# Second block of a two-block layer: loads in a written order, the swapped state rows from TensorE, one gelu batch, low weight parts by subtraction

## Chip, cores and metric

One Trainium2 chip, one of its cores. The metric is the device time of one execution in microseconds (us), the median of three runs.

## What is computed

Two transformer-like blocks follow each other on x (512 tokens, 1024 features, float32). The first block is not touched. The second one is, cut to what matters here:

```python
for l in range(DEPTH):
    h = _rms(x, norm1_w[l]) * (1 + sc1) + sh1
    u, q, k, v = jnp.split(h @ w_in[l], [...], axis=-1)
    y_ssm = _s5(u, ...)                       # state space layer, then z * sigmoid(z @ w_glu + b)
    y_attn = _swa_sink(q, k, v, rel_bias, sinks[l])   # 128-token window, 8 heads, 2 KV heads
    mixed = jnp.concatenate([_rms(y_ssm, ...), _rms(y_attn, ...)], axis=-1)
    x = x + g1 * (mixed @ w_out[l])
    h2 = _rms(x, norm2_w[l]) * (1 + sc2) + sh2
    x = x + g2 * _conv_ffn(h2, w_up[l], conv_w[l], conv_b[l], w_down[l])

def _s5(u, ...):        # 32 groups of 16 channels, 64 complex states each
    bu_re = einsum("blgh,gph->blgp", ug, bb_re)   # and bu_im
    s_re, s_im = associative_scan(s[t] = a * s[t-1] + bu[t])   # a complex
    y = einsum(s_re, c_re) - einsum(s_im, c_im) + d_skip * ug
    z = jax.nn.gelu(y)
    return z * jax.nn.sigmoid(z @ w_glu + b_glu)
```

## The kernel before

Features stand on the partitions and tokens in the columns. A product with a weight matrix is made of three float32 products of rounded parts: every weight tile `raw` (128x1024, loaded on SP's queue, two buffers) is split into a rounded part `whi` (ACT copies it, L367) and a rest `wlo`. There are five buffers of each. The rest is made in one of two ways in `load`: VectorE subtracts `whi` from `raw` (L373), or, for the matrices named in `DMA_LO`, ACT writes `-raw` rounded (L370) and a DMA issued by GpSimd reads the weights a second time and adds them to it (L371). The matrices are w5 (projections of the second block), w6 (the GLU), w7 (output projection), w8 (up projection, 44 tiles, read as 128x8x128) and w9 (down projection); before, w6, w7 and w8 have their rest from the DMA.

Between the first block's feed-forward part and the second one's lie the state space layer and the attention. There TensorE's order is written out by hand in `ORDER`, step by step; what the other engines do is put in order by the scheduler from the order in which the steps are written and from its own estimate of their times. The state space steps run over four quarters q of 8 groups: `a` multiplies the inputs `ua` with the table `et` (8 products of 64 columns) and copies the result to `z`, whose upper 64 rows are real parts and lower 64 rows imaginary ones. `b` rotates z by a table of cosines `co` and sines `si` (the sines multiply the rows exchanged between the halves, two instructions of 64 rows each in `crossed`, L1457 and L1458; the cosine product is GpSimd's) and scans (8 scans of 64 columns). `c` rotates back into `sp`. `d` makes y from the tables `tt`, `gt` (two buffers) and sp, copies it to `ys`, writes it to memory as eight small DMAs (`d_z`, half of them issued by SP, half by ACT) and reads it back rearranged as `yt`, to which d times u is added (L1498). `e` is the gelu of yt, which is `zT`, and its split `zhl`, in two batches of two. `g` is the GLU on it, in four parts, and `R` the norm that needs all four.

The attention steps: `kp`, `qp` project, `kt`, `qt` transpose to heads (after a norm of the tokens, `tokn`, on VectorE), `s` makes the scores of one block of 128 queries in two `sc` banks and adds the bias table `relb` on VectorE (L1589), ACT takes the exponentials, `t` transposes, `v` multiplies with the values, `p` is the output projection of the state space part. There are three PSUM banks `acc`, two `sc`, two `tr` and one `po`. `U` is the last projection of u; its copies go to memory (`d_u`) and come back as `ua` through 16 small DMAs of GpSimd.

After that comes `norm_tail` and the second feed-forward part, whose hidden units are made by `hidden2`.

Of the kernel before, what the change touches and what calls it, by code (L numbers as in the profile page):

```python
# [17 lines left out]
P = 128  # L18
# [23 lines left out]
HP = ""  # L42
EG = 0
EN = "avaaavaaaaaaaaaaaaavvvvvvvavavvaaaavaaaaaaaaaaaavaavvvvavvvvaaaavvvvaavvvaaaaavavaaavaavvavvvvvvvvvvavvaavvvvvavvaaavaaaavaaavvaaaaaaavvvvvvvaaaaaaaaavvvavvaavaaaav"
EN_AT = {'k1': (0, 4), 'v1': (4, 4), 'q1': (8, 12), 'h1': (20, 8), 'w1': (28, 8), 's1': (36, 8), 'o1': (44, 16), 't1': (60, 46), 'u2': (106, 4), 'z2': (110, 4), 'y2': (114, 4), 'k2': (118, 2), 'v2': (120, 2), 'q2': (122, 4), 'h2': (126, 12), 's2': (138, 12), 't2': (150, 14)}
ORDER = "U kp0 kp1 a0 a1 kt0 b0 qp0 c0 a2 b1 qp1 kt1 b2 c1 d0 a3 c2 qt0 qt1 b3 c3 d1 s0 qp2 s1 s2 t0 d2 t1 d3 e0 s3 e1 qt2 t2 s4 qp3 v0 t3 s5 v1 g0 qt3 g1 g2 t4 g3 s6 v2 v3 s7 t5 R p0 p1 v4 p2 t6 v5 p3 p4 v6 t7 p5 v7 p6 p7 A"
NW = 16
NHL = 5
SUM_E = "vector"
DMA_LO = ("w6", "w7", "w8")  # L50
LAG = 4
# [3 lines left out]
KSQ = 4  # L55
ZC = "bc"
UL = "gggggggggggggggg"
# [175 lines left out]
def build(tc, I, out, PV, PVN, CS, CSN, CS1, CSN1):  # L233
# [845 lines left out]
    def s5_tables():  # L1079
# [70 lines left out]
        V.tensor_copy(ro_r[:, 0], uc)  # L1150
        V.tensor_copy(ro_i[:, 0], us)
        for n in range(8):
# [237 lines left out]
    def tab(nm):  # L1390
        return bp.tile([P, 1024], F32, tag="tab", bufs=6, name=nm)
# [3 lines left out]

    def s5_load(qs):
        for q in qs:
            ets[q] = tab("et")
            nc.sync.dma_start(ets[q], d_et[q])
            cs[q], ss[q] = wt("co"), wt("si")  # L1400
            nc.sync.dma_start(cs[q], d_rot[q][:, 0])
            nc.sync.dma_start(ss[q], d_rot[q][:, 1])

    def s5_load2(qs):
        for q in qs:
            tts[q] = tab("tt")
            nc.sync.dma_start(tts[q], d_t[q].rearrange("p g x -> p (g x)"))
            gts[q] = bp.tile([P, 8, 9 * 16], F32, tag="tabg", bufs=2, name="gt")
            nc.sync.dma_start(gts[q].rearrange("p g x -> p (g x)"), d_g[q])

    s5_load((0, 1))
    s5_load2((0, 1))
    s5_load((2, 3))

# [32 lines left out]
    def s5_a(q):  # L1447
        pw = acc()
        for g in range(8):
            mm(pw[:, g * 64:g * 64 + 64], ets[q][:, g * P:(g + 1) * P], ua[:, q * 8 + g], True, True)  # L1450
        zs[q] = wt("z")
        copy("z2", q, zs[q], pw)

    def crossed(dst, src, t, sign):

        re, im = slice(0, 64), slice(64, 128)
        V.scalar_tensor_tensor(dst[re], src[im], sign, t[im], op0=ALU.mult, op1=ALU.mult)  # L1457
        V.scalar_tensor_tensor(dst[im], src[re], -sign, t[re], op0=ALU.mult, op1=ALU.mult)  # L1458

    def s5_b(q):  # L1460
        z, z2 = zs[q], wt("z2")
        z2s[q] = z2
        crossed(z2, z, ss[q], 1.0)
        zc = wt("zc")
        (G if "b" in ZC else V).tensor_tensor(zc, z, cs[q], op=ALU.mult)
        V.tensor_tensor(z, zc, z2, op=ALU.add)
        for g in range(8):
            c = slice(g * 64, g * 64 + 64)
            V.tensor_tensor_scan(z2[:, c], mag8[:, q * 8 + g:q * 8 + g + 1].to_broadcast([P, 64]), z[:, c], 0.0, ALU.mult, ALU.add)  # L1469

    def s5_c(q):
        if q == 2:
            s5_load2((2, 3))
        z, z2 = zs[q], z2s[q]
        crossed(z, z2, ss[q], -1.0)
        zc = wt("zc")
        (G if "c" in ZC else V).tensor_tensor(zc, z2, cs[q], op=ALU.mult)
        sp = bp.tile([P, 8, 65], F32, tag="sp", bufs=2, name="sp")
        sps[q] = sp
        V.memset(sp[:, :, 0:1], 0.0)  # L1480
        V.tensor_tensor(sp[:, :, 1:65], z.rearrange("p (g c) -> p g c", g=8),
                        zc.rearrange("p (g c) -> p g c", g=8), op=ALU.add)

    def s5_d(q):
# [6 lines left out]
        ys = wt("ys").rearrange("p (g c) -> p g c", g=8)  # L1491
        copy("y2", q, ys.rearrange("p g c -> p (g c)"), py)
        for t in range(8):
# [7 lines left out]
    def s5_e(n):  # L1501
        if EG and n == 0:
            return
        for q in (range(4) if EG else (2 * n, 2 * n + 1)):
            ge = act(zT[q], zT[q], AF.Gelu_apprx_tanh)
            zz = hl()
            split(zz, zT[q])
            zhl.append(zz)
        tables(ge)
# [139 lines left out]
    def ssm_out(k):  # L1649
# [7 lines left out]

    steps = dict(U=u_last, a=s5_a, b=s5_b, c=s5_c, d=s5_d, e=s5_e, kp=kv_p, kt=kv_t, qp=q_p, qt=q_t,
                 s=swa_s, t=swa_t, v=swa_v, g=glu, R=norm_s, p=ssm_out, A=norm_a)
    with tc.manual_schedule(engines={mybir.EngineType.PE}):  # L1660
        for step in ORDER.split():
            name = step.rstrip("0123456789")
            with tc.high_priority() if name in HP.split(",") else nullcontext():
                steps[name](*([int(step[len(name):])] if step != name else []))
# [93 lines left out]
```

## Time and profile before

| | us |
|---|---|
| median of three runs | 1289.39 |
| lowest, highest | 1288.81, 1290.92 |
| the profiled execution, its own time | 1290.49 |
| its span in the trace | 1288.8 |
| TensorE busy | 1229.4 (95% of the span) |
| VectorE busy | 839.0 (65%) |
| ScalarE busy | 553.6 (43%) |
| GpSimd busy | 319.7 (25%) |
| granted TensorE clock, mean | 0.974 |

The profile shows one execution. PE is TensorE, PEld its weight loads, DVE VectorE, ACT ScalarE, POOL GpSimd, SP the queue that issues most loads. Times in the rows are microseconds from the start of the span unless they are marked ns. The granted clock is a share of 2.4 GHz: 1.00 is the upper level and 0.50 the lower one, 1.2 GHz. A name behind an arrow (<-) is what the engine waited for last.

### The profile page before, as it was taken

The page shows a single profiled execution, that of the slowest core. Times are in us where ns is not written, and L with a number is a line of the kernel's source. Part 1 is how long each engine was busy: PE and PEld are TensorE (multiplying, and loading weights), DVE is VectorE, ACT ScalarE, POOL GpSimd, SP SyncE. Part 2 cuts the span into 40 slices and gives each one's busy share as a digit, 9 for nine tenths or more (in the row PEclk, how much of TensorE's full clock was granted, in tenths as well). Part 3 has the DMA queues.
Part 4 walks back from the last instruction along what each step waited for, and adds up shares of the span by engine and source line. Part 5 has one row for each costly group of instructions (what it writes and reads, how often), then busy time and mean ns, then how long its engine had stood idle before and what let it go on. Part 6 is the DMA issues. An engine that isn't in the chain of part 4 may idle for free.

```text
span 1288.8 us, 17279 instructions
## 1 busy us (share of the span) xinstructions
PE 1229.4 (95%) x6269; PEld 993.2 (77%) x6269; DVE 839.0 (65%) x1617; ACT 553.6 (43%) x917; POOL 319.7 (25%) x403
## 2 busy tenths in 40 slices
PE   6999999999999999999999979889799999999998
PEld 5878766567887888888889878668777788888887
DVE  7667858778977967677568497756547344434362
ACT  5424566453333323232325334765645544444430
POOL 3000002203408384664301231022121211111200
PEclk8999999999999999999999887989899999999999
DMA  6441111115356665656546873556799989796921
GB/s 219 136 135 50 51 33 50 50 41 172 125 177 200 202 213 177 207 182 198 176 142 233 249 181 106 138 135 125 144 205 199 211 166 162 147 178 139 189 82 66
DMA packets 211013, 192.96 MB, mean 150 GB/s; under 512 B 13040, under 2 KB 173696, under 8 KB 210928
## 3 DMA queue, kind: packets, MB, share of 16 engines
q1 hardware_dynamic: 154384, 146.96, 37.6%
q0 software_dynamic: 51456, 40.61, 19.8%
q10 hardware_dynamic: 5088, 4.29, 1.0%
q8 instruction: 50, 0.82, 0.3%
q14 instruction: 35, 0.29, 0.1%
HBM read 178.22 MB, written 15.43 MB: 150 GB/s over the span
## 4 chain that ended last, share of the span: by engine, by line
PE 68%; DVE 6%; issue 3%; DMA 3%; ACT 2%; POOL 1%; POOLq 0%; ACTq 0%; DVEq 0%
PE acc L261 48%; PE sc L261 10%; PE tr L261 8%; DMA wlo<-in_w_dram 2%; DMA raw<-in_w_dram 1%; PE po L261 1%; PE tr L1607 1%; DVE z L1469 1%; DVE wlo L373 1%; DVE z L1458 1%; DVE z L1457 1%; DVE wm L1073 0%; POOL wlo L371 0%; ACT prob L1596 0%; PE tr L932 0%
## 5 line engine op out<-in xcount | busy, mean ns | idle before, releaser
L261 PE MATMUL acc<-hl,whi 128*128 128x512 f32 (+1 forms) x1624 | 482.8, 380 | 11.4 <-ACT whi L367 7.3
L367 ACT ACTIVATE whi<-raw 128x1024 fp32r<-128x1024 f32 (+1 forms) x187 | 194.1, 1040 | 387.9 <-PE acc L261 235.9
L261 PEld LDWEIGHTS acc<-hl,whi 128*128 128x128 f32 x1624 | 294.5, 189 | 78.0 <-issue 8.8
L261 PE MATMUL acc<-hl,wlo 128*128 128x512 f32 (+1 forms) x812 | 308.1, 380 | 1.0 <-DMA wlo<-in_w_dram 1.0
L373 DVE TENSOR_TENSOR wlo<-raw,whi 128x1024 fp32r<-128x1024 f32 (+1 forms) x133 | 174.5, 1314 | 64.4 <-ACT whi L367 61.4
L261 PEld LDWEIGHTS acc<-hl,wlo 128*128 128x128 f32 x812 | 152.9, 188 | 32.8 <-issue 3.8
L371 POOL DMA_DIRECT2D wlo<-in_w_dram x54 | 72.0, 1334 | 323.9 <-ACT wlo L370 214.4
L261 PE MATMUL acc<-hd,whi 128*128 128x512 f32 (+1 forms) x472 | 143.1, 386 | 2.1 <-DVE x L1339 2.1
L261 PE MATMUL acc<-whi,hl 128*128 128x256 f32 (+1 forms) x544 | 109.0, 292 | 1.6 <-ACT tok L248 1.6
L261 PEld LDWEIGHTS acc<-hd,whi 128*128 128x128 f32 x472 | 86.9, 188 | 21.7 <-issue 3.1
L261 PEld LDWEIGHTS acc<-whi,hl 128*128 128x128 f32 x544 | 89.2, 195 | 6.1 <-ACT tok L248 3.0
L261 PE MATMUL acc<-hd,wlo 128*128 128x512 f32 (+1 forms) x236 | 90.9, 385 | 0.0
L1073 DVE CUSTOM_DVE_ANT_0 wm<-wm,cb 128x512 f32<-128x512 f32 x96 | 75.5, 818 | 12.1 <-DMA wm<-in_wmod_dram 12.1
L261 PE MATMUL acc<-wlo,hl 128*128 128x256 f32 (+1 forms) x272 | 78.8, 290 | 0.5 <-DVE wlo L373 0.5
L261 PE MATMUL tr<-hl,whi 128*128 128x512 f32 (+1 forms) x240 | 75.6, 398 | 0.0
L261 PE MATMUL sc<-hl,whi 128*128 128x512 f32 x208 | 64.9, 393 | 0.0
L370 ACT ACTIVATE wlo<-raw 128x1024 fp32r<-128x1024 f32 x54 | 56.5, 1047 | 4.1 <-DMA raw<-in_w_dram 2.2
L920 POOL TENSOR_SCALAR_AFFINE_SELECT keep<-keep 128x128 f32<-128x128 f32 x16 | 9.3, 594 | 186.6 <-ACT keep L914 185.8
L261 PE MATMUL tr<-hl,wlo 128*128 128x512 f32 (+1 forms) x120 | 48.0, 400 | 7.6 <-DMA wlo<-in_w_dram 7.6
L261 PEld LDWEIGHTS acc<-wlo,hl 128*128 128x128 f32 x272 | 53.1, 195 | 2.6 <-DVE wlo L373 1.0
L261 PEld LDWEIGHTS tr<-hl,whi 128*128 128x128 f32 x240 | 46.3, 196 | 10.3
L261 PEld LDWEIGHTS acc<-hd,wlo 128*128 128x128 f32 x236 | 44.3, 188 | 9.4
(424 smaller groups left out, 1962.3 us busy)
## 6 DMA issues: line engine op xcount, KB each, us to landing
raw<-in_w_dram SPq DMA_DIRECT2D x177, 512.0 KB, 4.4
wlo<-in_w_dram POOLq DMA_DIRECT2D x54, 512.0 KB, 7.9
wm<-in_wmod_dram SPq DMA_DIRECT2D x96, 256.0 KB, 4.0
xk<-in_xT_dram SPq DMA_DIRECT2D x16, 256.0 KB, 4.7
d_g<-s5g POOLq DMA_DIRECT2D x4, 576.0 KB, 4.4
gt<-d_g SPq DMA_DIRECT2D x4, 576.0 KB, 5.9
w1c<-in_w1k_dram SPq DMA_DIRECT2D x8, 256.0 KB, 6.4
w1c<-in_w1v_dram SPq DMA_DIRECT2D x8, 256.0 KB, 6.8
```

Source lines behind the costliest of these rows:

```text
L261: nc.tensor.matmul(o, lhsT=l, rhs=r, start=start, stop=stop, **k)
L367: act(hi[:, :m], raw[:, :m], AF.Copy)
L370: act(lo[:, :m], raw[:, :m], AF.Copy, scale=-1.0)
L371: nc.gpsimd.dma_start(v(lo), self.src[:, k0:k1, c0:c1], accum_op=ALU.add)
L373: V.tensor_tensor(lo[:, :m], raw[:, :m], hi.bitcast(F32)[:, :m], op=ALU.subtract)
L920: G.affine_select(g[:, d], g[:, d], fill=1.0, **past)
L1073: V.tensor_tensor_reduce(wm, wm, cb[:, n * 512:(n + 1) * 512], 1.0, 0.0, ALU.mult, ALU.add, mh[:, n, j:j + 1])
L1457: V.scalar_tensor_tensor(dst[re], src[im], sign, t[im], op0=ALU.mult, op1=ALU.mult)
L1458: V.scalar_tensor_tensor(dst[im], src[re], -sign, t[re], op0=ALU.mult, op1=ALU.mult)
L1469: V.tensor_tensor_scan(z2[:, c], mag8[:, q * 8 + g:q * 8 + g + 1].to_broadcast([P, 64]), z[:, c], 0.0, ALU.mult, ALU.add)
L1607: nc.tensor.transpose(tp[:, m * P:(m + 1) * P], probs[n][:, hh, (j - j0) * P:(j - j0 + 1) * P], ident)
```

## The change

Five edits, all in the second block. (1) SP's loads are put into TensorE's written order: `L` loads et, co and si of one quarter, `M` its tt and gt, `W` (`ahead`) the next weight tile; w5 goes ahead of most tables. (2) `a` also makes the rows exchanged between the halves, by 16 products of 64 rows into an `sc` bank, and `b` multiplies both banks with VectorE straight from PSUM; the sign of the sines is put into the table once (L1151). GpSimd keeps only the cosine product of `c`. (3) In `ORDER`, kt0 goes between a0 and a1, and `b1` ahead of `a2`, `c1` ahead of `b2`, `d1` ahead of `c3`. (4) The gelu of all four quarters is one batch (`EG`), behind the copy of the last y on ACT; all four copies of y are ACT's. (5) w8's rest is VectorE's difference.

```diff
-EG = 0
+EG = 1
...
-ORDER = "U kp0 kp1 a0 a1 kt0 b0 qp0 c0 a2 b1 qp1 kt1 b2 c1 d0 a3 c2 qt0 qt1 b3 c3 d1 s0 qp2 s1 s2 t0 d2 t1 d3 e0 s3 e1 qt2 t2 s4 qp3 v0 t3 s5 v1 g0 qt3 g1 g2 t4 g3 s6 v2 v3 s7 t5 R p0 p1 v4 p2 t6 v5 p3 p4 v6 t7 p5 v7 p6 p7 A"
+ORDER = "U L0 kp0 L1 kp1 M0 a0 kt0 a1 b0 qp0 L2 c0 M1 b1 a2 W qp1 W L3 kt1 c1 b2 W d0 a3 W M2 c2 qt0 qt1 b3 d1 c3 M3 s0 qp2 s1 s2 t0 d2 t1 d3 e0 s3 e1 qt2 t2 s4 qp3 v0 t3 s5 v1 g0 qt3 g1 g2 t4 g3 s6 v2 v3 s7 t5 R p0 p1 v4 p2 t6 v5 p3 p4 v6 t7 p5 v7 p6 p7 A"
...
-DMA_LO = ("w6", "w7", "w8")
+DMA_LO = ("w6", "w7")
...
-ZC = "bc"
+ZC = "c"
...
-        V.tensor_copy(ro_i[:, 0], us)
+        V.tensor_scalar(ro_i[:, 0], us, sgn, -1.0, op0=ALU.mult, op1=ALU.mult)
...
-    s5_load((0, 1))
-    s5_load2((0, 1))
-    s5_load((2, 3))
+    def s5_load(q):
+        ets[q] = tab("et")
+        nc.sync.dma_start(ets[q], d_et[q])
+        cs[q], ss[q] = wt("co"), wt("si")
+        nc.sync.dma_start(cs[q], d_rot[q][:, 0])
+        nc.sync.dma_start(ss[q], d_rot[q][:, 1])
+
+    def s5_load2(q):
+        tts[q] = tab("tt")
+        nc.sync.dma_start(tts[q], d_t[q].rearrange("p g x -> p (g x)"))
+        gts[q] = bp.tile([P, 8, 9 * 16], F32, tag="tabg", bufs=2, name="gt")
+        nc.sync.dma_start(gts[q].rearrange("p g x -> p (g x)"), d_g[q])
+
+    def ahead():
+
+        next(p_ for p_ in queue if p_.parts is None).load()
 
...
     def s5_a(q):
-        pw = acc()
+
+        pw, px = acc(), sc()
         for g in range(8):
-            mm(pw[:, g * 64:g * 64 + 64], ets[q][:, g * P:(g + 1) * P], ua[:, q * 8 + g], True, True)
-        zs[q] = wt("z")
-        copy("z2", q, zs[q], pw)
-
-    def crossed(dst, src, t, sign):
-
-        re, im = slice(0, 64), slice(64, 128)
-        V.scalar_tensor_tensor(dst[re], src[im], sign, t[im], op0=ALU.mult, op1=ALU.mult)
-        V.scalar_tensor_tensor(dst[im], src[re], -sign, t[re], op0=ALU.mult, op1=ALU.mult)
+            c, u = slice(g * 64, g * 64 + 64), ua[:, q * 8 + g]
+            mm(pw[:, c], ets[q][:, g * P:(g + 1) * P], u, True, True)
+            for r0 in (0, 64):
+                mm(px[r0:r0 + 64, c], ets[q][:, g * P + 64 - r0:g * P + 128 - r0], u, True, True, skip_group_check=True)
+        zs[q] = pw, px
 
     def s5_b(q):
-        z, z2 = zs[q], wt("z2")
-        z2s[q] = z2
-        crossed(z2, z, ss[q], 1.0)
-        zc = wt("zc")
-        (G if "b" in ZC else V).tensor_tensor(zc, z, cs[q], op=ALU.mult)
-        V.tensor_tensor(z, zc, z2, op=ALU.add)
+
+        pw, px = zs[q]
+        z, z2 = wt("z"), wt("z2")
+        V.tensor_tensor(z, pw, cs[q], op=ALU.mult)
+        V.tensor_tensor(z2, px, ss[q], op=ALU.mult)
+        V.tensor_tensor(z, z, z2, op=ALU.add)
         for g in range(8):
             c = slice(g * 64, g * 64 + 64)
             V.tensor_tensor_scan(z2[:, c], mag8[:, q * 8 + g:q * 8 + g + 1].to_broadcast([P, 64]), z[:, c], 0.0, ALU.mult, ALU.add)
+        zs[q], z2s[q] = z, z2
 
     def s5_c(q):
-        if q == 2:
-            s5_load2((2, 3))
+
         z, z2 = zs[q], z2s[q]
-        crossed(z, z2, ss[q], -1.0)
         zc = wt("zc")
         (G if "c" in ZC else V).tensor_tensor(zc, z2, cs[q], op=ALU.mult)
+        re, im = slice(0, 64), slice(64, 128)
+        V.scalar_tensor_tensor(z[re], z2[im], 1.0, ss[q][im], op0=ALU.mult, op1=ALU.mult)
+        V.scalar_tensor_tensor(z[im], z2[re], 1.0, ss[q][re], op0=ALU.mult, op1=ALU.mult)
         sp = bp.tile([P, 8, 65], F32, tag="sp", bufs=2, name="sp")
         sps[q] = sp
         V.memset(sp[:, :, 0:1], 0.0)
         V.tensor_tensor(sp[:, :, 1:65], z.rearrange("p (g c) -> p g c", g=8),
                         zc.rearrange("p (g c) -> p g c", g=8), op=ALU.add)
+
+    yc = [None]
 
     def s5_d(q):
         ut = wt("ut")
...
             mm(py[:, g * 64:g * 64 + 64], tts[q][:, g * P:(g + 1) * P], ua[:, q * 8 + g], True, False)
             mm(py[:, g * 64:g * 64 + 64], gts[q][:, g, 16:144], sps[q][:, g, 0:64], False, True)
         ys = wt("ys").rearrange("p (g c) -> p g c", g=8)
-        copy("y2", q, ys.rearrange("p g c -> p (g c)"), py)
+        yc[0] = act(ys.rearrange("p g c -> p (g c)"), py, AF.Copy)
...
         for q in (range(4) if EG else (2 * n, 2 * n + 1)):
-            ge = act(zT[q], zT[q], AF.Gelu_apprx_tanh)
+            with tc.issue_after(yc[0].ins):
+                ge = act(zT[q], zT[q], AF.Gelu_apprx_tanh)
...
-    steps = dict(U=u_last, a=s5_a, b=s5_b, c=s5_c, d=s5_d, e=s5_e, kp=kv_p, kt=kv_t, qp=q_p, qt=q_t,
+    steps = dict(L=s5_load, M=s5_load2, W=ahead, U=u_last, a=s5_a, b=s5_b, c=s5_c, d=s5_d, e=s5_e, kp=kv_p, kt=kv_t, qp=q_p, qt=q_t,
-    with tc.manual_schedule(engines={mybir.EngineType.PE}):
+    with tc.manual_schedule(engines={mybir.EngineType.PE, mybir.EngineType.SP}):
```

Three places show how the instructions move. The first is TensorE at the step a0, behind the projection kp1 (et is the table, ua the input):

```order
 L261 MATMUL acc<-wlo,hl 128x256
 L261 MATMUL acc<-whi,hl 128x256
-L261 MATMUL acc<-ua,et 128x64 x16
+L261 MATMUL acc<-ua,et 128x64
+L261 MATMUL sc<-ua,et 64x64 x2
```

Eight products of a quarter become eight of 128 rows and sixteen of 64 rows, taking turns.

The second is VectorE ahead of the first scores, s0, whose bias is added by the rows of L1589. Before:

```order
L1481 TENSOR_TENSOR sp_7225<-z_7062,zc_7223 128x8x64
L1457 SCALAR_TENSOR_TENSOR z2_7242<-z_7211,si_6695 64x512
L1458 SCALAR_TENSOR_TENSOR z2_7242<-z_7211,si_6695 64x512
L1589 ISA prob2_7301,ml_7298<-sc_7302,relb_7295 128x128
L1589 ISA ml_7298 128x1
L1466 TENSOR_TENSOR z_7211<-zc_7245,z2_7242 128x512
```

and now:

```order
L532 TENSOR_TENSOR tokn_7455<-tok_7454,nr_7461 128x512
L1497 SCALAR_TENSOR_TENSOR yt_7364<-ut_7335,pv_82,yt_7364 128x512
L1576 TENSOR_SCALAR relb_7378<-relb_7378 128x1024
L1589 ISA prob2_7384,ml_7381<-sc_7385,relb_7378 128x128
L1589 ISA ml_7381 128x1
```

Before, the scores of s0 stood among the rotations of quarter 3; now they stand behind the addition to yt of quarter 1 (L1497), which has to come back from memory first, and behind the sign change of the bias.

The third is ACT behind the copy of the last y. Before:

```order
L248 ACTIVATE ys_7519<-acc_7502 128x512
L499 ACTIVATE hl_7537<-yt_7292 128x512
L1495 DMA d_z3_3134<-ys_7519 16x8x64 x4
L311 ACT_TABLE_LOAD
L1594 ACTIVATE se_7543<-se_7543 128x4
L1596 ACTIVATE prob2_7544,sl_7542<-prob2_7544,ml_7541 128x256 x4
L1505 ACT_TABLE_LOAD
L1505 ACTIVATE yt_7483<-yt_7483 128x512
L248 ACTIVATE pt_7586<-tr_7581 128x512
L499 ACTIVATE hl_7566<-yt_7483 128x512
L1505 ACTIVATE yt_7529<-yt_7529 128x512
L311 ACT_TABLE_LOAD
```

and now:

```order
L1494 DMA d_z3_3134<-ys_7589 16x8x64 x4
L1596 ACTIVATE prob2_7605,sl_7603<-prob2_7605,ml_7602 128x256 x3
L1505 ACT_TABLE_LOAD
L1505 ACTIVATE yt_7261<-yt_7261 128x512
L1505 ACTIVATE yt_7364<-yt_7364 128x512
L499 ACTIVATE hl_7627<-yt_7261 128x512
L499 ACTIVATE hl_7631<-yt_7364 128x512
L1505 ACTIVATE yt_7553<-yt_7553 128x512
L1505 ACTIVATE yt_7599<-yt_7599 128x512
L499 ACTIVATE hl_7635<-yt_7553 128x512
L499 ACTIVATE hl_7639<-yt_7599 128x512
L311 ACT_TABLE_LOAD
```

The copy `pt` of a transposed tile and the exponentials of the next scores stood between the gelus; now they stand behind the whole batch, whose last gelu needs quarter 3 back from memory.

## Rows read from the trace of the kernel before

**Rows 1.** The page, busy us (share of the span) and instructions.

```profile
PE 1229.4 (95%) x6269; PEld 993.2 (77%) x6269; DVE 839.0 (65%) x1617; ACT 553.6 (43%) x917; POOL 319.7 (25%) x403
```

**Rows 2.** Who waited for whom on PE: us in total, times, longest us.

```profile
PE tr L261 <- DMA wlo<-in_w_dram: 7.6, 2, 5.8
PE sc L261 <- DVE ml L1589: 7.5, 3, 6.0
...
PE tr L1540 <- DVE tokn L532: 6.5, 1, 6.5
...
PE acc L261 <- DMA wlo<-in_w_dram: 1.0, 1, 1.0
```

**Rows 3.** Busy time by stretch: us, PE PEld DVE ACT POOL, PEclk, DMA share, GB/s.

```profile
920.00:1010.00 90.00, 80.82 (x337) 64.50 (x336) 42.78 (x82) 44.85 (x56) 18.70 (x13) 0.94 1.07 206
1010.00:1100.00 90.00, 90.00 (x390) 73.10 (x389) 42.99 (x55) 44.67 (x55) 15.80 (x11) 1.00 0.91 171
```

**Rows 4.** Busy time by stretch: the first feed-forward part, and the second.

```profile
300.00:500.00 200.00, 197.33 (x883) 158.51 (x882) 162.00 (x303) 65.94 (x88) 103.65 (x138) 1.00 0.60 182
930.00:1100.00 170.00, 166.62 (x707) 134.28 (x706) 81.03 (x130) 83.00 (x102) 31.63 (x22) 0.98 0.97 187
```

**Rows 5.** Groups by line and form: busy us, mean ns, idle before.

```profile
L373 DVE TENSOR_TENSOR wlo<-raw,whi 128x1024 fp32r<-128x1024 f32 x123 | 166.1, 1353 | 63.0 <-ACT whi L367 60.0 <-ACT rg L504 2.4
...
L370 ACT ACTIVATE wlo<-raw 128x1024 fp32r<-128x1024 f32 x54 | 56.5, 1047 | 4.1 <-DMA raw<-in_w_dram 2.2 <-PE acc L261 2.0
```

**Rows 6.** Timeline of PE: start us, us, what, count, idle before.

```profile
733.14 5.93 PE L261 MATMUL acc<-ua,et 128*128 128x64 f32 x32 [2.62 <-DMA raw<-in_w_dram]
...
746.04 1.89 PE L261 MATMUL acc<-ua,et 128*128 128x64 f32 x16
...
767.02 1.09 PE L1540 MATMUL tr<-cst,tokn 128*128 128x128 f32 x4 [6.51 <-DVE tokn L532]
...
775.67 1.23 PE L261 MATMUL sc<-k2T,q2T 64*128 64x128 f32 x8
...
783.56 1.94 PE L261 MATMUL sc<-k2T,q2T 64*128 64x256 f32 x8
...
802.06 0.39 PE L261 MATMUL acc<-sp,gt 128*128 128x64 f32 x2
...
842.34 2.07 PE L261 MATMUL sc<-k2T,q2T 64*128 64x256 f32 x4 [6.02 <-DVE ml L1589]
...
846.10 1.49 PE L261 MATMUL sc<-tot_s,cst 128*128 128x512 f32 x2
```

**Rows 7.** Busy time by stretch, around the step d1.

```profile
770.00:780.00 10.00, 10.00 (x54) 9.66 (x54) 7.70 (x24) 0.60 (x1) 3.89 (x3) 0.56 0.38 106
```

**Rows 8.** Groups of PE by form, narrow weights: busy us, mean ns.

```profile
L261 PE MATMUL po<-pt,vtok 128*64 128x128 f32 x88 | 7.7, 284 | 0.0
...
L261 PE MATMUL sc<-s5g,bb 128*16 128x128 f32 x64 | 2.5, 275 | 0.0
```

**Rows 9.** DMA issues by line: KB each, median us to landing.

```profile
yt<-d_z POOLq DMA_DIRECT2D x4, 256.0 KB, 3.0
...
d_z<-ys ACTq DMA_DIRECT2D x16, 32.0 KB, 2.2
```

**Rows 10.** Timeline of ACT: start us, us, what, count, idle before.

```profile
776.45 2.02 ACTq L1495 DMA_DIRECT2D d_z<-ys  x4
...
810.48 0.58 ACT L248 ACTIVATE pt<-tr 128x512 f32<-128x512 f32 x1
...
813.87 1.28 ACT L311 ACT_TABLE_LOAD   x1
...
837.63 1.06 ACT L367 ACTIVATE whi<-raw 128x1024 fp32r<-128x1024 f32 x1 [4.55 <-DMA raw<-in_w_dram]
```

**Rows 11.** Timeline of PE where 64-row products give way to 128-row ones.

```profile
816.12 1.08 PE L261 MATMUL po<-pt,v 128*64 128x256 f32 x8
817.13 0.73 PE L261 MATMUL acc<-hl,whi 128*128 128x512 f32 x2
```

More of the change, by code (lines that the diff above doesn't have):

```diff
@@ L1394, in build @@
     zs, z2s, cs, ss, sps, ets, tts, gts = {}, {}, {}, {}, {}, {}, {}, {}
[L1396 to L1409, printed above, removed]
-    s5_load((0, 1))
-    s5_load2((0, 1))
-    s5_load((2, 3))
+    def s5_load(q):
[11 more added lines that the diff above has]
+        next(p_ for p_ in queue if p_.parts is None).load()
     def u_out(q, ps):
```

## The prediction

> **What bounds the kernel now.** I read the page first: PE is busy 1229.4 us of a span of 1288.8 [rows 1], so 59.4 us of PE idle, and whatever a low clock costs inside the busy time, is all that any edit can win, unless it takes products away; this one adds some. Then the list of who waited for whom on PE: of its largest waits four lie in the second block, 7.6 and 1.0 us for a rest tile that comes by DMA, 7.5 us for the row minimum of the scores and 6.5 us for the normed tokens [rows 2]. The table by stretch shows what the first two cost in all: in 920 to 1010 PE did 337 instructions at a mean granted clock of 0.94, in the next 90 us 390 of the same kind at 1.00 [rows 3]. The timeline of PE shows where the others lie [rows 6]: 6.51 us ahead of the transposes of qt1 at 767.02, and 6.02 us ahead of s7 at 842.34. Around the first, PE is busy but slow: in 770 to 780 the granted clock was 0.56, near the lower level of 1.2 GHz, after the wait [rows 7]. The sum below is made against the profiled execution, 1290.49 us, which is 1.1 us over the median of the runs, 1289.39; I carry the difference over unchanged.
>
> **w8's rest by subtraction: -12.2 us.** Removed: 44 of the 54 ACT instructions of 1.05 us that write -raw [rows 5], 44 issues on GpSimd and 44 tiles of 512 KB read a second time. Added: 44 subtractions on VectorE, 1.35 us each by the mean of its group, 60 us [rows 5]. VectorE was busy 81 of 170 us in 930 to 1100; with about 1.35 us for each of some 26 tiles there it comes to 116 of 170, 68%. In the first feed-forward part, where every rest is already subtracted, VectorE was busy 162 of 200 us and PE 197 of 200 [rows 4]: that load does not hold PE up. What hides the subtractions is thus VectorE's own slack; should it go, each one late costs up to 1.35 us. The two tiles that follow the norm come behind its last instruction on VectorE instead of behind a DMA. The gain is the 53 missing instructions of 920 to 1010 at 90/390 = 0.23 us: 12.2 us, of which 8.6 are waits [rows 2, 3] and the rest mostly low clock. Bounds: -12.2, and -2 if the load of raw itself, two buffers deep, was the real limit. I take the full value, since DMA engines were busy 1.07 there and half of w8's reading goes away.
>
> **The start, 0 us.** SP now brings the next w5 tiles ahead of most tables, but ACT's queue has the issue of the last `d_u` ahead of the second tile of kv, which can hold up kp0 by some 2 us. PE waited 2.62 us ahead of a0 anyway [rows 6], for inputs that go through memory. One covers the other: 0, between -2.6 and +2.
>
> **The exchanged rows on PE: +12.4 us.** 64 products of 64 rows are added, two instructions each as for the others, 128. A full one took 5.93/32 = 0.185 us at the low clock of 733 and 1.89/16 = 0.118 at the high one, a ratio of 1.57 [rows 6]. No row has this shape. From above it is the full one at the low clock throughout, 0.185: 23.7 us. From below it is weights of 16 columns, 2.5/64 = 0.039 each: 5.0 us [rows 8]. Nearest are weights of 64 columns with twice as many columns streamed, 7.7/88 = 0.088 [rows 8]; I take a little less, 0.08. Those of a0 and half of a1, 48, fall where PE was slow: 48 x 0.08 x 1.57 = 6.0; the other 80 cost 6.4. They lie on PE's path, since nothing there waits for another engine now. VectorE loses the two 64-row products of `b` and gains two of 128 rows; with the two copies of z it had and GpSimd's product gone, `b` is shorter.
>
> **The wait at qt1: -10.9 us.** qt0 ended at 767.02 - 6.51 = 760.51, and s0 began at 775.67 [rows 6]: 15.2 us for the 4 transposes of qt1 and the 32 instructions of d1. At 0.118 they need 4.25. In VectorE's new order the rotation of quarter 1 stands behind the norm of qp0 and ahead of the norm of qp1, and PE has kt1, d0 and a longer a3 between qp1 and qt1, so the tokens are there. Bounds: -10.9, and -6.5 if the clock stays low.
>
> **A new wait at s1: +4.3 us.** The scores of s0 hold both `sc` banks until VectorE has added the bias, and that now stands behind the addition to yt of quarter 1. From the end of d1: ACT's copy of y, then a weight tile's two conversions (2.1 us [rows 5]) and the issue of the writes (2.02 [rows 10]), 2.2 us to land, the read back 3.0 [rows 9], and five short instructions (copy, GpSimd's issue, addition, sign of the bias, products of one bank), which I estimate at the 0.58 us of a 128x512 copy on ACT each [rows 10], 2.9: 12.2 us. Before, s1 began 783.56 - 775.67 = 7.9 us after d1 [rows 6], and PE comes there no later now. Queued behind that addition on VectorE are all scores and, through them, t0 and d2. Bounds: 0 (the conversions run earlier), and +9.5 (both transfers take twice as long).
>
> **One gelu batch, and s7: -3.5 us.** The 7.5 us that PE waited for ml [rows 2], 6.02 of them ahead of s7 [rows 6], go nearly whole: ACT stood at 837.63 for 4.55 us before a weight tile that had just been asked for [rows 10], with the split that VectorE needed behind it; in the new order on SP and ACT that tile is asked for several tiles earlier. That is -7.0. But the copy `pt`, at 810.48 before, 8.0 us after the end of d3 (802.45) [rows 6, 10], now stands behind the batch: copy 0.6, issue 2.0, landing 2.2, issue 0.6, landing 3.0, addition 0.6, gelu 0.6, two splits 1.2, all estimates or rows as above, and a table load of 1.28 [rows 10], 12.1; and ahead of it five small instructions for the exponentials of s3, at the same 0.58, 2.9: 15.0 us, 7.0 later. PE's work between covers an unknown part; half is +3.5. Bounds of the whole: -7.0 and +7.0.
>
> **Norm before the second feed-forward part: +0.5 us.** Three subtractions (4.1 us) stand among its chain on VectorE and three conversions leave ACT. VectorE waited for PE and ACT there; I let one eighth through. Bounds 0 and +4.1.
>
> Sum: -12.2 + 0 + 12.4 - 10.9 + 4.3 - 3.5 + 0.5 = -9.4. The profiled execution would take 1281.1 us, the median 1280.0. The forecast's own range is 1272 to 1288.
>
> **Rivals.** (a) *The stage gains in full.* The narrow products run side by side at the lower price (5.0), yt comes back in time (0), and the batch is free (-7.0): -12.2 + 5.0 - 10.9 - 7.0 + 0.5 = -24.6, 1264.8 us. For it: the price of the narrowest weights in rows 8. Against it: VectorE's order is fixed with yt ahead of the scores, and a write and a read back cannot take nothing.
>
> (b) *Slower: PE drains at each change of width.* Full and half products take turns, 64 changes over the four quarters (two per group). If each one waits until the product before it is through, it costs the difference between the length of one and its pitch, 0.284 - 0.088 = 0.197 us [rows 8]: 12.6 us, at the steps a, on PE's path. Then the sum is +3.2, 1292.6 us. It decides against the change from 0.15 us per switch (9.4/64). Against it: where eight half-width products give way to full ones, these start at 817.13, before the 1.08 us from 816.12 are over [rows 11]; one change shows no gap. For it: no row has them taking turns. The Trainium skill, "TensorEngine Tiling (Array Packing)", section "Tiling Modes", Key Properties, says that a change of the tiling mode drains TensorE, and that tiles of one mode work independently; the switch in rows 11 does not show the former at a size that matters, and by the page this change would pay it 64 times.
>
> (c) *The second feed-forward part keeps its wait.* If the stall at its start was that of raw, not of the second read, only 2 of the 12.2 us go: +0.8, 1290.2 us. For it: raw has two buffers. Against it: the first feed-forward part has the same buffers and loses 3 us in 200.
>
> **Chances.** Forecast 0.53, (a) 0.22, (b) 0.15, (c) 0.10. A measurement of this kernel can tell about 0.2%, 2.6 us, from no change. Faster by more than that: nine tenths of the forecast's, all of (a), a tenth or two of (b) and (c), 0.74. Within it: 0.13. Slower: 0.13, nearly all from (b). The range 1264 to 1293 reaches from (a) to (b); outside it are sums at two bounds at once.
>
> **What would show it.** Right: no wait of PE for wlo after the norm, and about 390 instructions in the 90 us that begin w8; a0 to a3 with 0.13 us per half product at first and 0.08 later; no wait at qt1; a wait of about 4 us at s1 put down to ml; t3 waiting for pt, s7 not waiting. Wrong: half products over 0.15 us each at the high clock; PE waiting in the second feed-forward part for VectorE's wlo; or the stage from a0 to R shorter than before by over 10 us.

## Result and the profile after

The changed kernel takes **1304.04 us**, median of 9 runs (1292.46 to 1310.17), beside 1290.34 for the kernel before on the same chips (9 runs, 1288.81 to 1295.84). The ratio is **1.008, 95% interval 1.0055 to 1.0106**: slower by about 10 us (7 to 14). The forecast was 1280.0, faster, with a range of 1264 to 1293; the time lies outside it and the sign is wrong. Times below that come from a ratio are the ratio's distance from 1 times 1290 us.

The two profiled executions, 1305.97 and 1290.49 us, differ by 15.5 us. Where it arises is read from PE's timeline. After:

```profile
734.32 0.33 PE L261 MATMUL acc<-ua,et 128*128 128x64 f32 x2
...
734.85 0.43 PE L261 MATMUL acc<-ua,et 128*128 128x64 f32 x2
735.21 0.34 PE L261 MATMUL sc<-ua,et 128*64 128x64 f32 x4
735.48 0.44 PE L261 MATMUL acc<-ua,et 128*128 128x64 f32 x2
...
776.91 1.97 PE L1540 MATMUL tr<-cst,tokn 128*128 128x128 f32 x8
...
785.53 1.22 PE L261 MATMUL sc<-k2T,q2T 64*128 64x128 f32 x4
789.28 1.19 PE L261 MATMUL sc<-k2T,q2T 64*128 64x128 f32 x4 [2.53 <-DVE z L1460]
804.30 2.49 PE L261 MATMUL sc<-k2T,q2T 64*128 64x256 f32 x8 [5.94 <-DVE ml L1589]
...
848.52 1.97 PE L1607 MATMUL tr<-cst,prob 128*128 128x128 f32 x8 [7.11 <-ACT pt L248]
...
871.75 1.83 PE L261 MATMUL sc<-k2T,q2T 64*128 64x256 f32 x8 [2.80 <-DVE ml L1589]
...
875.27 1.80 PE L261 MATMUL sc<-tot_s,cst 128*128 128x512 f32 x2
```

Against [rows 6]: a0 begins at 734.32, 1.2 us later than before; s0 at 785.53 instead of 775.67, 9.9 later; s1 at 804.30 instead of 783.56, 20.7 later; R at 875.27 instead of 846.10, 29.2 later. So the stretch from a0 to s1 loses 20 us and that from s1 to R another 8. In what follows R, the span gives 13.8 of the 29.2 back (1304.2 against 1288.8 at its end): that is w8, by the stretches of 90 us that begin it, to be held against the 337 and 390 instructions and the clocks of 0.94 and 1.00 in [rows 3]:

```profile
949.00:1039.00 90.00, 90.00 (x397) 73.47 (x397) 68.45 (x109) 41.48 (x54) 0.00 (x0) 1.00 0.55 161
1039.00:1129.00 90.00, 90.00 (x390) 73.14 (x390) 51.71 (x62) 32.79 (x41) 0.00 (x0) 1.00 0.33 96
```

The list of who waited for whom on PE, after, against [rows 2]: the rest by DMA is gone from it, and so is tokn ahead of qt1. The scores' minimum (ml) stands at 8.7 us instead of 7.5; new are pt with 7.1 and z with the 2.53 of the rows above.

```profile
PE sc L261 <- DVE ml L1589: 8.7, 2, 5.9
...
PE tr L1607 <- ACT pt L248: 7.1, 1, 7.1
```

Last the clock. By stretches of 30 us from 760, before:

```profile
760.00:790.00 30.00, 21.06 (x119) 19.12 (x117) 26.52 (x77) 8.40 (x30) 9.53 (x10) 0.70 0.51 148
790.00:820.00 30.00, 28.21 (x189) 25.02 (x188) 22.43 (x73) 21.64 (x51) 1.07 (x2) 0.85 0.32 89
820.00:850.00 30.00, 21.36 (x99) 15.48 (x99) 22.54 (x55) 24.61 (x54) 3.46 (x4) 0.83 0.72 172
```

and after:

```profile
760.00:790.00 30.00, 27.47 (x176) 25.76 (x175) 15.77 (x39) 8.60 (x15) 5.90 (x7) 0.67 0.62 154
790.00:820.00 30.00, 23.45 (x111) 21.04 (x110) 17.30 (x59) 7.80 (x31) 4.19 (x5) 0.61 0.31 96
820.00:850.00 30.00, 21.97 (x121) 19.53 (x120) 13.96 (x40) 11.96 (x31) 1.10 (x2) 0.67 0.44 123
```

The waits are shorter in the first of them (PE busy 27.47 instead of 21.06), yet the clock is lower in all three: behind each new wait PE goes on at 1.2 GHz (granted clock 0.50 from 801.7 to 835.9, from 846.1 to 852.9 and from 873.4 to 876.8). From s2 to the end of d3 the same work took 19.6 us (807.41 to 827.00) instead of 16.4 (786.02 to 802.38).

### The profile page after: what moved, and what is told of

It is laid out like the page before. It is cut to its first block, busy times and chain, and to the rows that moved or that the text cites. A ratio compares the mean times of both kernels' runs of the same rounds, so it can differ in the third digit from the quotient of the medians.

```text
span 1304.2 us, 17370 instructions
## 1 busy us (share of the span) xinstructions
PE 1254.9 (96%) x6397; PEld 1014.8 (78%) x6397; DVE 886.8 (68%) x1658; ACT 507.0 (39%) x868; POOL 251.5 (19%) x355
## 5 line engine op out<-in xcount | busy, mean ns | idle before, releaser
L373 DVE TENSOR_TENSOR wlo<-raw,whi 128x1024 fp32r<-128x1024 f32 (+1 forms) x177 | 232.3, 1315 | 97.9 <-ACT whi L367 93.7
L261 PE MATMUL acc<-whi,hl 128*128 128x256 f32 (+1 forms) x544 | 117.0, 306 | 2.5 <-ACT tok L248 1.6
L261 PEld LDWEIGHTS acc<-whi,hl 128*128 128x128 f32 x544 | 95.8, 210 | 7.4 <-ACT tok L248 3.0
L261 PE MATMUL acc<-wlo,hl 128*128 128x256 f32 (+1 forms) x272 | 82.7, 304 | 1.4 <-DVE wlo L373 1.4
L261 PE MATMUL tr<-hl,whi 128*128 128x512 f32 (+1 forms) x240 | 72.9, 386 | 0.0
L261 PEld LDWEIGHTS acc<-wlo,hl 128*128 128x128 f32 x272 | 57.0, 210 | 3.6 <-DVE wlo L373 2.1
L1339 DVE TENSOR_TENSOR x<-x,acc 128x512 f32<-128x512 f32 (+1 forms) x49 | 31.7, 655 | 22.4 <-PE acc L261 22.3
L261 PEld LDWEIGHTS sc<-hl,whi 128*128 128x128 f32 x208 | 39.1, 188 | 9.0
```

Of the source, the lines that this page charges most:

```text
L261: nc.tensor.matmul(o, lhsT=l, rhs=r, start=start, stop=stop, **k)
L373: V.tensor_tensor(lo[:, :m], raw[:, :m], hi.bitcast(F32)[:, :m], op=ALU.subtract)
L1339: done[0] = V.tensor_tensor(x[k][:, cs], x[k][:, cs], ps[:, cs], op=ALU.add)
```

## Experiments: the parts alone

Four kernels each add one part of the change to the kernel before.

**w8's rest by subtraction.**

```diff
-DMA_LO = ("w6", "w7", "w8")
+DMA_LO = ("w6", "w7")
```

> The kernel before with the one edit that w8's low parts are differences (DMA_LO without w8). Theory: this part does in the second feed-forward part what the term of the prediction says, since the changed kernel's stretch from the end of the norm to the end is 13.9 us shorter than before's; 10 to 15 us faster than before, about 1277 us, and no wait of PE for wlo after the norm. Rival: the gain shows only because the changed kernel comes to this stretch with other loads in flight; then 0 to 5 us faster.

Measured: 1277.75 us, ratio 0.9904 (0.988 to 0.9927), 12.4 us faster. In the 90 us that begin w8 PE issued 405 instructions at full clock, where [rows 3] has 337:

```profile
920.00:1010.00 90.00, 90.00 (x405) 73.78 (x404) 68.56 (x109) 41.05 (x52) 0.00 (x0) 1.00 0.51 156
```

The term stands, at its size.

**The exchanged rows.** The edits to `s5_a`, `s5_b`, `s5_c`, to `ZC` and to the sign of the table, without any other.

> The kernel before with the exchanged rows from the matrix engine alone (loads, order of steps, gelu and w8 as before). Theory A (the loss sits in the rows): 128 instructions at the 0.095 us each that the changed kernel's a0 shows at the high clock, 12 us, and more where the clock falls during them, as it does in a1, a2 and a3 there; with nothing of the wait at qt1 gone, since before's order puts qt1 right behind qt0: 12 to 25 us slower, 1302 to 1315 us. Theory B (the loss sits in the new order and the waits for yt): the shorter b on VectorE gives part of the 6.5 us at qt1 back, so 3 to 9 us slower.

Measured: 1301.18 us, ratio 1.0082 (1.0062 to 1.0103), 10.6 us slower, between the two theories and nearer to A; its interval, 8 to 13, reaches into the ranges of both, so it doesn't decide between them. The wait of 6.5 us at qt1 is gone here too (`b` is shorter on VectorE), and still the sum is a loss.

**The gelu batch.** `EG = 1`, the copies of y on ACT, the gelu behind the last of them.

> The kernel before with the one gelu batch alone (EG=1, the copy of y on ScalarE, gelu issued after the last copy). Theory B (the batch makes t3 wait for the last yt): PE waits 5 to 8 us ahead of t3 for pt and no longer 6.0 us ahead of s7: between 2 us faster and 6 us slower. Theory A (the batch is free): the wait ahead of s7 goes, 4 to 7 us faster.

Measured: 1291.48 us, ratio 1.0002 (0.998 to 1.0023): no difference. PE's waits show both halves of it, 3.3 us for pt ahead of t3 (not there before) and 2.9 in all for ml, where the list before has 7.5:

```profile
PE tr L1610 <- ACT pt L248: 3.3, 1, 3.3
PE sc L261 <- DVE ml L1592: 2.9, 3, 1.7
```

**The loads and the order of steps.** `ORDER`, `L`, `M`, `W` and SP in the written order.

> The kernel before with the fixed order of loads on SP and the new order of steps alone (state rows as before, two gelu batches, w8 as before). Theory A (the loss sits in the rows): the wait at qt1 goes, 5 to 11 us faster. Theory B (the order brings yt of quarter 1 late to the scores): s1 waits 4 to 10 us for ml, and what qt1 gave is lost again: 0 to 10 us slower than before.

Measured: 1305.98 us, ratio 1.0119 (1.0097 to 1.0142): 15.4 us slower, more than either theory gave. Alone it is the dearest part. It holds the loads (1) and the exchanged steps of `ORDER` (3) together; which of the two makes the loss was not tried apart. s0 comes 4.2 us earlier than before (771.48 against 775.67), and s1 9.8 later:

```profile
771.48 1.23 PE L261 MATMUL sc<-k2T,q2T 64*128 64x128 f32 x8
793.35 2.49 PE L261 MATMUL sc<-k2T,q2T 64*128 64x256 f32 x8 [13.17 <-DVE ml L1585]
```

The four parts add up to -12.4 + 10.6 + 0.2 + 15.4 = +13.8 us. The whole change measured 10 (7 to 14). So most of the loss lies in two of the parts, and they can be looked into one by one. Some interplay is left: taken out of the changed kernel, the rows give back about 7 us and an early bias table 3.6 by the ratios (both below), where alone these two are worth 10.6 and 10.3.

## Experiments: what makes the order of loads dear

The search begins with SP's queue. In the kernel before, the scheduler asked for the bias table at 748.0 us, some 28 us ahead of s0:

```profile
747.96 0.33 SPq L1575 DMA_DIRECT2D relb<-in_relb_dram  x1
```

In the written order its load stands where the step s0 stands, behind the tables of quarter 3 (`M3`) and, ahead of these, SP's half of the writes of y of quarter 1, which need ACT's copy of the result of d1. SP is held at these writes; the tables and relb follow without another wait. After:

```profile
786.26 1.94 SPq L1494 DMA_DIRECT2D d_z<-ys  x4
788.51 0.34 SPq L1405 DMA_DIRECT2D tt<-d_t  x1
788.95 0.79 SPq L1407 DMA_DIRECT2D gt<-d_g  x1
789.79 0.42 SPq L1575 DMA_DIRECT2D relb<-in_relb_dram  x1
```

Then yt of quarter 1 is read back. GpSimd can ask for that read only behind the cosine product of c3, which waits for b3's scan. That scan is late because VectorE stood 9.09 us at the clearing of `sp` for quarter 3: `sp` has two buffers, and the one needed comes free when d1 has read quarter 1's. The rest of c2 and all of b3 come behind that on VectorE. VectorE has its sign change of relb and the scores behind the norm of the tokens of qp2 and the addition to that yt. GpSimd's timeline, the DMA issues of relb and of that yt (KB, us to landing) and VectorE's timeline, after:

```profile
791.61 1.71 POOL L1471 TENSOR_TENSOR zc<-z,co 128x512 f32<-128x512 f32 x1 [11.66 <-DVE z L1464]
793.27 0.90 POOL L371 DMA_DIRECT2D wlo<-in_w_dram  x1
793.87 0.86 POOL L1496 DMA_DIRECT2D yt<-d_z  x1
```

```profile
relb<-in_relb_dram SPq DMA_DIRECT2D x1, 512.0 KB, 5.2
...
yt<-d_z POOLq DMA_DIRECT2D x1, 256.0 KB, 5.5
```

```profile
785.68 0.07 DVE L1477 MEMSET sp<- 128x8 f32 x1 [9.09 <-PE acc L261]
...
799.02 0.69 DVE L519 TENSOR_TENSOR nsq<-tok 128x512 f32<-128x512 f32 x1 [3.77 <-ACT tok L248]
...
801.64 0.69 DVE L532 TENSOR_TENSOR tokn<-tok,nr 128x512 f32<-128x512 f32 x1
802.25 0.74 DVE L1497 SCALAR_TENSOR_TENSOR yt<-ut,pv,yt 128x512 f32<-128x512 f32 x1
802.92 0.69 DVE L1576 TENSOR_SCALAR relb<-relb 128x1024 f32<-128x1024 f32 x1
803.73 0.29 DVE L1589 CUSTOM_DVE_ANT_0 prob<-sc,relb 128x128 f32<-128x128 f32 x1
```

The read takes 5.5 us, where the yt row of [rows 9] has 3.0, and is there at about 799.4. The tables had landed by then (the later one at 793.8); beside it travelled the end of relb, a weight tile's rest and two reads of u. VectorE still has the norm of qp2 ahead of the addition, and PE's qp2, which ends at 798.4 and ran at the low clock until 794.9, lets that norm begin only at 799.02. So the scores of s0, all in PSUM by 790.5, begin at 803.73.

Two things thus hold the scores back. relb is there at 795.0, and before that they can't begin; that is the smaller one. VectorE changes its sign only at 802.92, 7.9 us later: that is its place in VectorE's order. In b_loads relb is there at 788.3 and its sign is changed at 791.6, behind a wait of 6.0 us for yt.

The test is to ask for relb earlier and change no other load; since its sign change then comes earlier in the written order too, the scheduler also puts the scores of s0 and s1 ahead of most of the norm and of that addition on VectorE.

```diff
-... W L3 kt1 c1 ...
+... W L3 B0 kt1 c1 ...
...
+    def relb_load(kv):
+        t = tab("relb")
+        relbs[kv] = t.rearrange("p (h y) -> p h y", h=4)
+        nc.sync.dma_start(t, I["relb"][:, kv * 1024:(kv + 1) * 1024])
+        V.tensor_scalar(relbs[kv], relbs[kv], -1.0, None, op0=ALU.mult)
...
-        if i == 0:
-            relbs[kv] = tab("relb").rearrange("p (h y) -> p h y", h=4)
...
+        if i == 0 and kv not in relbs:
+            relb_load(kv)
...
```

> The kernel of b_loads with one step moved: the load of the position bias relb and its change of sign stand behind the load of the last et table instead of at s0, which is behind the tables of quarter 3. Theory C (the order of loads costs because relb, asked for at 748.0 us in the kernel before, is asked for only at 782 to 790, behind tables that wait for buffers until d1 ends, and because VectorE then has the addition to yt ahead of the scores): the wait of 13.2 us for ml ahead of s1 nearly goes, and the kernel is 9 to 15 us faster than b_loads, 1291 to 1297 us. Theory D (it is the slow read of yt itself, 4 to 7 us beside the tables): VectorE still waits for yt ahead of the scores, less than 4 us faster than b_loads.

Measured: 1294.68 us, ratio 1.0039 (1.0021 to 1.0056) against 1.0119 of b_loads: 10.3 us faster, theory C. SP asks for relb at 751.22, and PE's wait ahead of s1 falls from 13.17 to 2.54 us; s1 comes at 784.35, 9.0 earlier than in b_loads:

```profile
784.35 2.34 PE L261 MATMUL sc<-k2T,q2T 64*128 64x256 f32 x8 [2.54 <-DVE ml L1589]
```

The run moves the load and VectorE's order together; what each has of the 10.3 us was not tried apart. The same step in the changed kernel:

> The changed kernel with the same step moved. Theory C: the wait of 5.9 us for ml ahead of s1 goes, and with it the low clock behind it in t0, d2 and d3, 3 us; 6 to 12 us faster than the changed kernel, 1292 to 1298 us; the wait of t3 for pt stays. Theory D: less than 3 us faster.

Measured: 1295.75 us, ratio 1.0052 (1.0027 to 1.0076). By medians that is 8.3 us under the changed kernel, by the ratios 3.6, and the intervals overlap, so the total alone decides little. In the trace s1 comes at 794.40 instead of 804.30, with a wait of 1.83 instead of 5.94. But 5.9 of these 9.9 us stand already at the first products of s0 (779.62 instead of 785.53), ahead of any use of relb: in this run a2 went through at the high clock. From s0 to s1 it is 14.8 us instead of 18.8, so the trace gives the edit 4.0. The wait ahead of t3 stays, 7.8 us.

What is left of b_loads with relb cured, 5 us (3 to 7), was not taken apart. PE shows a wait of 3.4 us ahead of t0 there, and one of 4.6 for tokn ahead of qt1, where the kernel before has 6.5, so the latter isn't it.

## Experiments: what makes the rows dear

In the changed kernel two full products and four half ones take 0.63 us at the high clock (from 734.85 to 735.48, shown above). The full ones took 0.236 [rows 6], so a half one costs 0.1 if it carries the difference. The rival (b) says that it is the change of width. Grouping tells them apart:

```diff
-        for g in range(8):
-            c, u = slice(g * 64, g * 64 + 64), ua[:, q * 8 + g]
+        cu = [(slice(g * 64, g * 64 + 64), ua[:, q * 8 + g]) for g in range(8)]
+        for g, (c, u) in enumerate(cu):
             mm(pw[:, c], ets[q][:, g * P:(g + 1) * P], u, True, True)
+        for g, (c, u) in enumerate(cu):
             for r0 in (0, 64):
                 mm(px[r0:r0 + 64, c], ets[q][:, g * P + 64 - r0:g * P + 128 - r0], u, True, True, skip_group_check=True)
```

> The kernel of b_rows with the products of a step a in another order: the eight of full width first, then the sixteen of half width, so that the width changes twice in a quarter instead of sixteen times. Theory A (a change of width costs): the pair of full products behind the half ones takes 0.36 us instead of 0.236 at the high clock in the changed kernel, 0.124 us at each of 32 groups, so 3 to 5 us faster than b_rows, 1296 to 1298 us. Rival (the alternation costs nothing, the time is that of the columns): within 1.5 us of b_rows. A third: full drains of 0.197 us at 64 changes would give 11 to 12 us.

Measured: 1293.85 us, ratio 1.0028 (1.0016 to 1.0041): 7.0 us faster than b_rows, between the first and the third expectation. PE's timeline of a2 shows the prices apart:

```profile
749.05 1.89 PE L261 MATMUL acc<-ua,et 128*128 128x64 f32 x16
750.87 1.15 PE L261 MATMUL sc<-ua,et 128*64 128x64 f32 x32
751.95 0.39 PE L261 MATMUL acc<-whi,hl 128*128 128x256 f32 x1
```

Start to start, sixteen full ones take 1.82 us and 32 half ones 1.08, each run with the one change of width that ends it. Two full and four half ones that take turns need 0.63 us, with two changes. From these three sums come 0.104 us for a full one, 0.029 for a half one, under the lowest price of [rows 8], and **0.15 us for a change of width**, 9.8 us for 64. The starts inside the runs give nearly the same (a full one every 0.112 us, two half ones every 0.058): 0.145 us for a change, 9.3 for 64. My first expectation had seen only one of the two.

**Without the rows.** The changed kernel with `s5_a` to `s5_c`, `ZC` and the table's sign of before.

> The changed kernel with the state rows as before: crossed products on VectorE, the copy of z, no half products on the matrix engine. If the parts add up as they did alone (rows +10.6 us), 1292 to 1295 us. Rival: in the new order the rows are what takes the wait at qt1 away, and without them it comes back: 1298 us or more.

Measured: 1292.81 us, ratio 1.0024 (1.0011 to 1.0037), about 7 us under the changed kernel, as the parts say. The wait ahead of s1 is 12.1 us here: s0 comes 12.2 us earlier than in the changed kernel (773.38), and s1 10.2 (794.07), since the scores stand behind the same yt there, for which VectorE waits 4.9 us.

## Experiments: cures together, and the batch's place

**Both cures in the changed kernel**, relb early and the products grouped:

> The changed kernel with two cures: relb asked for behind the last et table (as a_relb) and half products behind all full ones of a quarter (as br_grp). If the cures add up: 7 us faster than a_relb, 1287 to 1291 us, about the kernel before. Rival: part of what the grouping gives is taken by the wait for pt ahead of t3 (7.8 us in a_relb), which follows yt and not PE: 1291 to 1294 us.

Measured: 1283.88 us, ratio 0.9933 (0.9909 to 0.9957): 8.6 us faster than the kernel before, better than expected. From a_relb it is 15.4 us by the ratios, 11.9 by the medians and 7.3 in the profiled spans (1291.5 and 1284.2), so what the grouping is worth here stays open between 7 and 15. In the trace the grouped products ran at the high clock in all four a steps, 2.9 us each. The wait for pt ahead of t3 stays at 7.9.

**w8 and the batch, without the rest:**

> The kernel before with two parts of the change: w8's low parts as differences and the one gelu batch. Parts that add up (-12.4 and +0.2 us alone): 1276 to 1280 us, not to be told from b_w8. Rival: the batch's wait for pt ahead of t3 (3.3 us in b_eg) is hidden or its gain at s7 (6.0 to 1.7 us) counts more once the weights come as differences: 1272 to 1275 us.

Measured: **1275.16 us, ratio 0.9874 (0.9853 to 0.9894)**, the lowest median of the study, between my two expectations: 16.3 us (14 to 19) under the kernel before. It is not surely under b_w8, whose interval overlaps.

**The batch behind t2.** t3 waits because the copies of t2 stand behind gelus that wait for the last yt. ACT, in the changed kernel:

```profile
844.88 0.63 ACT L1505 ACTIVATE yt<-yt 128x512 f32<-128x512 f32 x1 [6.05 <-DVE yt L1497]
845.42 1.13 ACT L499 ACTIVATE hl<-yt 128x512 fp32r<-128x512 f32 x2
846.57 1.28 ACT L311 ACT_TABLE_LOAD   x1
847.87 0.60 ACT L248 ACTIVATE pt<-tr 128x512 f32<-128x512 f32 x1
```

```diff
-... e0 s3 e1 qt2 t2 s4 ...
+... e0 s3 qt2 t2 e1 s4 ...
```

> The kernel of bw_eg with the gelu batch one place later in the order of steps, behind t2 instead of ahead of it, so that both copies pt of t2 stand ahead of the batch on ScalarE and VectorE. Theory (t3 waits because those copies stand behind a batch that waits for the last yt): the 3.3 us ahead of t3 go, 2 to 5 us faster than bw_eg, and the best of all, 1272 to 1276 us. Rival (the batch is then late for the gate's products): a wait of PE for hl ahead of g0 takes the place of t3's, within 1.5 us of bw_eg.

Measured: 1281.29 us, ratio 0.992 (0.9893 to 0.9948), 5.9 us slower than bw_eg. A miss: the wait ahead of t3 falls from 3.55 to 1.42 us, but 6.41 ahead of s7 are back, for the reason that [rows 10] show before: ACT stands before a weight tile (4.93 us, raw at 842.81) with what VectorE needs behind it.

```profile
816.97 1.06 PE L1610 MATMUL tr<-cst,prob 128*128 128x128 f32 x8 [1.42 <-DVE prob L1602]
...
847.51 2.07 PE L261 MATMUL sc<-k2T,q2T 64*128 64x256 f32 x4 [6.41 <-DVE ml L1592]
```

> The kernel of a_relb_grp with the gelu batch behind t2 in the order of steps. Theory as for bw_eg_t2: the wait of 7 to 8 us for pt ahead of t3 goes, 4 to 8 us faster than a_relb_grp, 1280 to 1286 us, faster than before but not than b_w8. Rival: g0 waits for hl instead, within 1.5 us.

Measured: 1283.2 us, ratio 0.9926 (0.9899 to 0.9952), the same as a_relb_grp. The 7.9 us ahead of t3 are 1.4 now, and 3.7 appear ahead of s5 for ml; R comes at 853.77 instead of 853.17. The rival's size held, not its place. That stretch does not end with the one wait that is largest in it.

## Why the prediction was wrong

**The step that failed is "A new wait at s1: +4.3".** It took 12.2 us from the end of d1 to s1, bounded at +9.5 by twice the transfers. The trace has 18.8 (785.5 to 804.30), against 7.9 before: +10.9, beyond its bound. No other term came out dearer than its dear bound. The direction and the queue were right (the scores behind the addition to yt on VectorE), but four things were left out. VectorE stood 9 us in front of the clearing of `sp` for quarter 3, with c2 and b3 behind it, so GpSimd, behind c3's product, issued the read only at 793.87, some 3 us after the writes were there (issued by 788.2, 2.2 us to land). The read then takes 5.5 us instead of 3.0. The norm of qp2, which stood ahead of the addition in the order I showed, holds the addition up to 802.25. And relb, asked for 42 us later than before, is there only at 795.0, so that scores ahead of the norm could not have begun before that either. bl_relb shows relb's place together with VectorE's order to be worth 10.3 us alone, and a_relb some 4 in the changed kernel; the others are read from the trace and were not tried alone. The start's term counted what SP's new order brings forward and not what it puts back.

**Exchanged rows, +12.4.** Right in sum, by luck. The four steps took 21.9 us instead of 9.2, +12.7. But a half product costs 0.03 us at the high clock, not 0.08, and some 9.5 us are changes of width. Rival (b)'s mechanism was there at about 0.15 us per change instead of 0.197, at the very price from which I had it decide; I had put the two in different cases, while the nearest row's price happened to cover half products and changes alike. The 0.185 us that I took as a full product's price at the low clock is a mean over a stretch whose clock fell only at 734.4; in d1, at 0.50, it was 0.214. Since the sum of the term came out, this is not why the forecast failed. I had judged the switch in [rows 11] by the overlap alone; the pair of products behind it takes 0.73 us, the next such pair 0.64, so some 0.1 us was there to be seen:

```profile
817.93 0.64 PE L261 MATMUL acc<-hl,whi 128*128 128x512 f32 x2
```

br_grp shows that a change costs time here. The Trainium skill's page "TensorEngine Tiling (Array Packing)", section "Tiling Modes", says that a change of the tiling mode drains TensorE. With that br_grp agrees in the cost; it does not show what TensorE does meanwhile.

Not in the term at all: `px` holds a bank of `sc` until VectorE has multiplied it, and s0 waits 2.5 us for that (1.5 in b_rows, 4.2 in a_relb_grp); in the changed kernel that product too stands behind the clearing of `sp`.

**The wait at qt1, -10.9.** The 6.5 us are gone, but qt0's and qt1's transposes and d1 (776.91 to 785.53) run at the low clock, 0.214 us an instruction in d1. With half of the 1.8 us of transposes qt1's, 7.7 us remain of 15.2: -7.5, near the bound of -6.5 and not the value taken.

**One gelu batch, -3.5.** In the changed kernel t3's wait grew by 7.1 and s7's (0.94 and 6.02) fell to 2.8: +2.9, within the bounds. Alone the part is worth nothing either way. Half of t3's wait covered by PE was a guess, and nothing covered it.

**w8, -12.2,** held (-12.4 alone, some 13.8 behind R). **The start, 0,** held: +1.2, with 0.9 us each for whi and wlo at kp0, as feared. **The norm, +0.5,** held: R to the first product behind the norm took 57.0 before (846.10 to 903.07) and 57.1 after (875.27 to 932.35).

The clock between the steps was put at nothing, without a reason; this is the other step that failed. There qp0 and qp1 took 16.3 us instead of 12.2, being behind the a steps during which it fell, and s2 to d3 3.2 us more. With these 7.3 us, which are read from one trace of each kernel, +10.9 in place of +4.3, -7.5 in place of -10.9 and +2.9 in place of -3.5, the sum of -9.4 becomes +14, close to the 15.5 between the profiled executions.

## What to carry to other kernels

When a load queue goes from a scheduler's order to a written one, list every load on it and compare when each is asked for before and after, above all those that the written steps mention only at their use. Then look where the scheduler puts the instructions that use them on the other engines: here relb came 42 us later on SP, but was there 7.9 us before VectorE's turn came to it, and moving both forward gave back 10.3 us in b_loads. When products of two widths are needed, issue each width in one run (7.0 us here). And a wait that was removed came back here at the next thing that PE waits for: in bw_eg_t2 t3's fell to 1.42 us and 6.41 stood ahead of s7.

## What the runs showed of the hardware

Half-width products (weights of 64 columns, 64 streamed) in a run take 0.029 us each at the high clock, less than a third of a full one (0.104 to 0.112); a change between the widths takes about 0.15 us there. At the low clock 32 of them with the change behind take 1.90 us (a1 of br_grp, granted clock 0.50) instead of 1.08. The granted clock fell to its lower level within runs of such small products although PE was never idle in them: in the changed kernel inside a1, a2 and a3. In a1 PE had done a0, four transposes and most of a1 at the high clock before it; by stretches, up to the fall and behind it:

```profile
733.00:743.72 10.72, 10.72 (x103) 8.83 (x101) 6.96 (x13) 3.37 (x6) 0.00 (x0) 1.00 1.03 257
743.80:745.20 1.40, 1.40 (x11) 1.09 (x10) 1.40 (x8) 0.00 (x0) 0.00 (x0) 0.50 1.00 403
```

PE's timeline there:

```profile
743.43 0.45 PE L261 MATMUL acc<-ua,et 128*128 128x64 f32 x2
743.81 0.48 PE L261 MATMUL sc<-ua,et 128*64 128x64 f32 x4
744.23 0.69 PE L261 MATMUL acc<-ua,et 128*128 128x64 f32 x2
744.85 0.48 PE L261 MATMUL sc<-ua,et 128*64 128x64 f32 x4
```

From a full pair to the next half ones it is 0.38 us in the first of these groups and 0.62 in the next, with no wait between. In a_relb the clock fell inside a1 too, but a2 went through at the high one, so it is not shown that the small products cause the fall. The changed kernel's runs lie 18 us apart where those of before lie within 7, and they go with the mean granted clock of the run: 0.977 at 1292.46 and 1293.67 us, 0.961 at 1309.73 and 1310.17. Why the clock differs from run to run stays open; at 0.977 the changed kernel is only 2 to 3 us over the one before.
